# Encoder layer on one core: the first tile's queries projected alone, the other three tiles' queries behind its attention

## The chip, the cores and the metric

The kernel runs on one core of a Trainium2 chip. The time is the device time of one execution in microseconds (us). The kernel before was run three times: 1670.38, 1673.27 and 1676.81 us, median 1673.27 us.

## What is computed

One layer of a bidirectional encoder on 512 tokens of width 1024, float32. The part that the change touches is the mixer:

```python
hn = rms_norm(h, g_mix)
c_q, c_kv, k_r, q_d, k_d, v_d = split(hn @ w_in)          # 384, 256, 32, 512, 512, 512 columns
q  = rms_norm(c_q, g_cq) @ w_uq                           # 8 heads x 96, the last 32 with rope
kv = rms_norm(c_kv, g_ckv) @ w_ukv                        # keys and values of 8 heads
o_mla = softmax(q k^T) v                                  # all 512 keys
o_dil = dilated_attention(rope(q_d), rope(k_d), v_d)      # here: a bias and one softmax over 512 keys
h = h + concat(rms_norm(o_mla), rms_norm(o_dil)) @ w_out
h = h + peer_ffn(rms_norm(h))                             # top 16 of 128 x 128 experts for each of 8 heads
h = h + sigmoid(rms_norm(h) @ w_gate) * (p @ w_proj)
out = rms_norm(h)
```

Keys and values need all four tiles of 128 tokens. The queries of a tile are used by that tile's attention alone.

## The kernel before, in words

The 512 tokens are four tiles of 128; `ORDER = [1, 2, 3, 0]` is the order in which they go through attention ("first tile" below is tile 1, "last tile" is tile 0). One TensorE (PE) does all matrix work; VectorE (DVE), ScalarE (ACT) and GpSimd (POOL) do the rest; SyncE (SP) issues the loads.

**Projections** (L284 to L357). Five groups of columns of `w_in` in the order kv, kd, cq, qd, vd. A group has 8 chunks of 128 rows; each chunk's weights are loaded (`load_piece`), split into a high part on ACT and a low part on DVE (`w_step`, L186 and L188), and used by three matmuls for each of the four tiles (`mm_step`, L194). After a group its sums are evicted (L345 to L349), and a generator (`post_latent`, `post_dil`) goes on with them step by step (`run_posts`) between the next group's chunks: norm, rope, transposes, and for cq the product with `w_uq` (L250) and the transposes into `qT` (L259).

**Attention** (`attention`, L488). For each tile 8 steps of two heads: four with `qT` (L422), four with `qd` (L425). A step is `scores` (two matmuls, DVE reduction, ACT exponential), `weigh` (L442, L444), `flip` (L451, 8 transposes) two steps later and `values_` (L466) three steps later. `finish` (L482) ends a tile and starts its `after` generator: 8 pieces of `w_out` (L523), norm, transposes (L545), 8 pieces of `w_pq` (L562), products with the keys (L574). The pieces come through a ring of `WQB = 4` buffers. Between the steps of attention the loop takes one step of the oldest `after` and calls `fill(us)`, which takes steps from a list of background work `bg`.

**Background work.** When `after` of a tile ends it appends `topk` (L606: MAX, FIND_INDEX and MATCH_REPLACE on DVE, then decoding and a softmax) and, for tiles 1, 2 and 3, four `gates` (L686: one-hot products B on DVE, L713; matmuls, L724; eviction, L727; a store into `gD`). `topk` of a tile ends with three transposes on PE (L669, L670). The gates of the third tile are barred (`PRE`) until the dense stage.

**Dense stage** (from L870). For 128 rows of experts, matmuls h (L870) and y (L896) on the gated tiles. It starts when `bg` holds nothing but what is barred.

The built program's order on each engine is not the order of the code: a scheduler moves instructions of an engine past one another. So the order is shown below as it is built.

Of the kernel before, what the change touches and what calls it, by code (L numbers as in the profile page):

```python
# [52 lines left out]
WQB = 4  # L53
# [17 lines left out]
def encoder_kernel(ctx, tc, x, xT, pT, w_in, w_uq, w_ukv, w_out, w_pq, keysT, u, v, uT, vB, w_gate, w_proj,  # L71
# [7 lines left out]
    wk_s = ExitStack()  # L79
    wk = wk_s.enter_context(tc.tile_pool(name="wk", bufs=2))  # L80
# [4 lines left out]

    def t4(shape, name):
        return wk.tile(shape, F32, tag="t4", name=name, bufs=3)

    def t2(shape, name):
        return wk.tile(shape, F32, tag="t2", name=name, bufs=6)  # L90
# [3 lines left out]
    nTh = pj.tile([P, NC, T], FR, name="nTh", bufs=1)  # L94
    nTl = pj.tile([P, NC, T], FR, name="nTl", bufs=1)
# [3 lines left out]
    def load_piece(name, c):  # L99
        c0, c1 = WCOLS[name]  # L100
        w = pj.tile([P, 512], F32, tag="w", name="w", bufs=3)[:, :c1 - c0]
        nc.sync.dma_start(w, w_in[c * P:(c + 1) * P, c0:c1])
        raw[name, c] = w

    def norm_chunk(c):
        xc = t2([P, T], "xc")
        nc.sync.dma_start(xc, xT[c * P:(c + 1) * P, :])
        g = gc[:, G_MIX + c:G_MIX + c + 1]
        nc.scalar.activation(nTh[:, c, :], xc, AF.Copy, scale=g)
        nc.vector.scalar_tensor_tensor(nTl[:, c, :], xc, g, nTh[:, c, :].bitcast(F32), op0=OP.mult, op1=OP.subtract)  # L110
# [5 lines left out]
    io = wk.tile([P, NK], F32, name="io")  # L116
# [19 lines left out]

    def rstd_of(sq, small, src, width, pre=None):
        ss = small.tile([P, 3], F32, tag="ss", name="ss", bufs=8)
        nc.scalar.activation(sq, src, AF.Square, accum_out=ss[:, 0:1], scale=1.0 if pre is None else pre)
        nc.vector.tensor_scalar(ss[:, 1:2], ss[:, 0:1], 1.0 / width, EPS, op0=OP.mult, op1=OP.add)  # L140
        nc.gpsimd.tensor_tensor(ss[:, 2:3], ss[:, 1:2], nhalf, op=OP.pow)
        return ss[:, 2:3]

    def junk(width):
        return t2([P, 512], "sq").bitcast(BF)[:, :width]
# [36 lines left out]
    def w_step(name, c):  # L182
        w = raw.pop((name, c))
        n = w.shape[1]
        wh = pj.tile([P, 512], FR, tag="wh", name="wh", bufs=2)[:, :n]
        nc.scalar.activation(wh, w, AF.Copy)  # L186
        wl = pj.tile([P, 512], FR, tag="wl", name="wl", bufs=2)[:, :n]
# [3 lines left out]
    def mm_step(c, acc, wh, wl):  # L191
        for t in range(NT):
            for k, (l, r) in enumerate(((nTl, wh), (nTh, wl), (nTh, wh))):
                nc.tensor.matmul(acc[t], l[:, c, tok[t]], r, start=(c == 0 and k == 0),  # L194
                                 stop=(c == NC - 1 and k == 2))
# [3 lines left out]
    cqT = pj.tile([P, 3, T], F32, name="cqT", bufs=1)  # L199
    W = {}  # L200

    def post_latent(src, n, g0, dst, kr):
        lat = []
        for t in range(NT):
            c = src[t]
            r = rstd_of(junk(n * P), wk, c[:, :n * P], n * P)
            nc.vector.tensor_scalar(c[:, :n * P], c[:, :n * P], r, None, op0=OP.mult)
            if kr:
                rope(c[:, n * P:][:, None, :], rm[:, t], 1, 16)
        yield  # L210
        for t in range(NT):
            ps = tp1()
            for k in range(n):
                nc.tensor.transpose(ps[:, k, :], src[t][:, k * P:(k + 1) * P], ident)
            if kr:
                nc.tensor.transpose(ps[:KR, n, :], src[t][:, n * P:n * P + KR], ident)
            mul_g(dst[:, :, tok[t]], ps[:, :n, :], g0, n)
            if kr:
                nc.scalar.activation(krT[:, tok[t]], ps[:KR, n, :], AF.Copy)
            if t % 2:  # L220
                yield
        if kr:
            for h in range(NH):
                if h % 2:
                    nc.scalar.activation(kkT[HD:QK, h, :], krT, AF.Copy)
                else:
                    nc.vector.tensor_copy(kkT[HD:QK, h, :], krT)
            yield
            for hp in range(NH // 2):
                ps = tp1().rearrange("p a b -> p (a b)")  # L230
                for c in range(2):
                    nc.tensor.matmul(ps, W["ukv"][:, c, hp * P:(hp + 1) * P], ckT[:, c, :], start=(c == 0), stop=(c == 1))
                for a in range(2):
                    nc.scalar.activation(kkT[:HD, 2 * hp + a, :], ps[a * HD:(a + 1) * HD, :], AF.Copy)
                if hp % 2:
                    yield
            for t in range(NT):
                ps = tp1().rearrange("p a b -> p (a b)")
                for c in range(2):
                    nc.tensor.matmul(ps, ckT[:, c, tok[t]], W["ukv"][:, c, 512:], start=(c == 0), stop=(c == 1))  # L240
                nc.scalar.activation(vv[:, 0, t, :], ps, AF.Copy)
                if t % 2:
                    yield
        else:
            for t in range(NT):
                qt = t4([P, NH, QK], "qt")
                for s in range(2):
                    ps = tp1().rearrange("p a b -> p (a b)")
                    for c in range(3):
                        nc.tensor.matmul(ps[:, :384], cqT[:, c, tok[t]], W["uq"][:, c, s * 384:(s + 1) * 384],  # L250
                                         start=(c == 0), stop=(c == 2))
                    nc.scalar.activation(qt[:, 4 * s:4 * s + 4, :].rearrange("p h d -> p (h d)"), ps[:, :4 * QK],
                                         AF.Copy, scale=MLA_SCALE)
                rope(qt[:, :, HD:], rm[:, t], NH, 16)
                yield
                for s in range(2):
                    ps = tp1()
                    for h in range(4):
                        nc.tensor.transpose(ps[:QK, h, :], qt[:, 4 * s + h, :], ident)  # L259
                    nc.scalar.activation(qT[:QK, 4 * s:4 * s + 4, tok[t]], ps[:QK], AF.Copy)  # L260

    def post_dil(src, dst):
        for t in range(NT):
            rope(src[t].rearrange("p (h d) -> p h d", h=NH)[:, :, :16], rd[:, t], NH, 8)
            if t % 2:
                yield
        for t in range(NT):
            ps = tp1()
            for c in range(4):
                nc.tensor.transpose(ps[:, c, :], src[t][:, c * P:(c + 1) * P], ident)  # L270
            nc.scalar.activation(dst[:, :, tok[t]], ps, AF.Copy)
# [3 lines left out]
    seq = [(n, c) for n in ("kv", "kd", "cq", "qd", "vd") for c in range(NC)]  # L275
    pos_ = [0]

    def prefetch(k):
        for _ in range(k):
            if pos_[0] < len(seq):  # L280
# [7 lines left out]
    rm = pj.tile([P, NT, 2, 32], F32, name="rm", bufs=1)  # L288
    rd = pj.tile([P, NT, 2, 16], F32, name="rd", bufs=1)
# [7 lines left out]
    def r1_of(t):  # L297
        xt = t4([P, D], "xt")
        nc.sync.dma_start(xt, x[tok[t], :])
        r = rstd_of(junk(D), wk, xt, D)  # L300
# [12 lines left out]
    nxt = None  # L313
    for gi, name in enumerate(("kv", "kd", "cq", "qd", "vd")):
        n = WCOLS[name][1] - WCOLS[name][0]
        acc = [mm1()[:, :n] for _ in range(NT)]
        for c in range(NC):
            if nxt is None:
                nxt = w_step(name, c)
            cur = nxt  # L320
            prefetch(1)
            if gi == 0:
# [4 lines left out]
                if c == 4:  # L327
                    misc_loads()
            k = gi * NC + c + 1
            nxt = w_step(*seq[k]) if k < len(seq) else None  # L330
            mm_step(c, acc, *cur)
            run_posts()
        if gi == 0:
# [3 lines left out]
        if name == "vd":  # L337
            for t in range(NT):
                nc.scalar.activation(vv[:, 1, t, :], acc[t], AF.Copy, scale=r1[:, t:t + 1])
        else:  # L340
            ev = []
            for t in range(NT):
                e = pj.tile([P, 512], F32, tag="ev", name="ev", bufs=4)[:, :n]
                if name == "qd":
                    nc.vector.tensor_scalar(e, acc[t], r1[:, t:t + 1], -DIL_SCALE, op0=OP.mult, op1=OP.mult)  # L345
                elif t % 2:
                    nc.vector.tensor_scalar(e, acc[t], r1[:, t:t + 1], None, op0=OP.mult)
                else:
                    nc.scalar.activation(e, acc[t], AF.Copy, scale=r1[:, t:t + 1])  # L349
                ev.append(e)  # L350
            posts.append({"kv": lambda: post_latent(ev, 2, G_CKV, ckT, True),
                          "kd": lambda: post_dil(ev, kd),
                          "cq": lambda: post_latent(ev, 3, G_CQ, cqT, False),
                          "qd": lambda: post_dil(ev, qd)}[name]())
            run_posts()
    while posts:
        run_posts()  # L357
    pj_s.close()
    ps1_s.close()

    wk_s.close()

    tk_s = ExitStack()
# [7 lines left out]
    wa_s = ExitStack()  # L371
    wa = wa_s.enter_context(tc.tile_pool(name="wa", bufs=2))
    ps2_s = ExitStack()
    psum = ps2_s.enter_context(tc.tile_pool(name="psA", bufs=4, space=bass.MemoryType.PSUM))
# [835 lines left out]
```

## Time and profile before

| | us |
|---|---|
| median of 3 runs | 1673.27 |
| the profiled execution | 1674.36 |
| its span, on which all times of the trace lie | 1672.3 |
| PE busy in the span | 1604.1 (96%) |
| DVE busy | 1223.8 (73%) |
| ACT busy | 737.5 (44%) |
| POOL busy | 372.6 (22%) |

A busy share is an average over stages with different limits. So the stages are read apart: the trace has the projections from 0 to 149.7 us, attention with the `after` work and the background from there to the last `finish` at 415.4 us, a tail of `after`, `gates` and `topk` until the first dense matmul at 501.7 us, and the dense stage behind that. In the trace's rows "PEclk" is the clock granted to PE, as a share of 2.4 GHz; "PEld" is its weight loads, which run beside its matmuls.

### The profile page before, as it was taken

The numbers are of one execution on the slowest core, as the hardware profiler recorded it, in microseconds if no ns is written. First come the engines' busy times: TensorE is split into PE (matmuls) and PEld (weight loads), VectorE is DVE, ScalarE is ACT, GpSimd is POOL, SyncE is SP. The second block draws the span as 40 slices with busy tenths as digits, with TensorE's granted clock in tenths as the row PEclk, the third lists the DMA queues.
The fourth block names the chain that finished last, engine by engine and source line by source line (L and its number), as shares of the span: only waits on it lengthen the run. The fifth ranks groups of instructions, "written<-read, shape, count | busy, mean of one in ns | idle before, by whom it ended". The sixth has DMA issues, their size and how long they took to land.

```text
span 1672.3 us, 24854 instructions
## 1 busy us (share of the span) xinstructions
PE 1604.1 (96%) x9369; PEld 1405.3 (84%) x9369; DVE 1223.8 (73%) x2495; ACT 737.5 (44%) x1220; POOL 372.6 (22%) x302
## 2 busy tenths in 40 slices
PE   7999999999679989999999999999999999999998
PEld 6776777778669889999999999999999999999877
DVE  5235468796999867787887887788888888864566
ACT  5435655645446544433333333333333333333455
POOL 1000000000000001044444444444444444300000
PEclk9999999999889999999999999999999999999999
DMA  7212254375867667599999999999999999975511
GB/s 240 62 52 95 82 172 133 114 239 206 298 248 243 233 216 265 185 309 327 324 321 323 309 334 321 324 316 339 320 312 313 334 322 323 319 269 200 182 58 51
DMA packets 154088, 402.73 MB, mean 241 GB/s; under 512 B 13168, under 2 KB 64496, under 8 KB 152432
## 3 DMA queue, kind: packets, MB, share of 16 engines
q1 hardware_dynamic: 115232, 241.48, 43.4%
q0 software_dynamic: 36864, 134.23, 23.3%
q10 hardware_dynamic: 1872, 25.43, 3.9%
q8 instruction: 73, 1.20, 0.3%
q14 instruction: 47, 0.39, 0.1%
HBM read 369.64 MB, written 31.46 MB: 240 GB/s over the span
## 4 chain that ended last, share of the span: by engine, by line
PE 82%; DVE 11%; ACT 2%; DMA 2%; issue 1%; POOL 1%; SPq 0%; POOLq 0%; DVEq 0%; ACTq 0%
PE y L896 31%; PE h L870 31%; PE mm L194 4%; PE mm L523 2%; PE mm L562 2%; PE pg L965 2%; PE po L466 2%; PE gq L724 2%; DVE B L713 1%; PE tp L451 1%; PE mm L425 1%; PE mm L422 1%; PE tp L250 1%; DVE rep L595 1%; DVE hot L709 1%
## 5 line engine op out<-in xcount | busy, mean ns | idle before, releaser
L870 PE MATMUL h<-xTh,lo 128*128 128x384 f32 (+1 forms) x1024 | 340.3, 332 | 0.8 <-ACT gt L673 0.8
L870 PE MATMUL h<-xTh,hi 128*128 128x384 f32 (+1 forms) x1024 | 340.1, 332 | 0.0
L870 PE MATMUL h<-xTl,hi 128*128 128x384 f32 (+1 forms) x1024 | 339.0, 331 | 0.0
L774 POOL DMA_INDIRECT row<-in_u_dram,ei x128 | 165.9, 1296 | 449.2 <-DVE row L762 241.4
L896 PE MATMUL y<-hi,wl 128*128 128x512 f32 x768 | 241.4, 395 | 8.5 <-DVE wl L885 8.5
L896 PE MATMUL y<-lo,wh 128*128 128x512 f32 x768 | 238.9, 392 | 0.0
L896 PE MATMUL y<-hi,wh 128*128 128x512 f32 x768 | 238.4, 392 | 0.0
L774 POOL DMA_INDIRECT row<-in_v_dram,ei x128 | 182.5, 1426 | 208.5 <-DVE h L768 170.1
L819 DVE TENSOR_TENSOR lo<-v,hi 128x1024 fp32r<-128x1024 f32 x140 | 171.5, 1225 | 73.4 <-ACT hi L817 72.8
L879 ACT ACTIVATE w<-h 128x384 f32<-128x384 f32 (+2 forms) x140 | 65.0, 464 | 361.6 <-PE h L870 346.6
L870 PEld LDWEIGHTS h<-xTh,lo 128*128 128x128 f32 x1024 | 193.8, 189 | 5.8 <-ACT gt L673 1.1
L870 PEld LDWEIGHTS h<-xTl,hi 128*128 128x128 f32 x1024 | 193.8, 189 | 4.7
L870 PEld LDWEIGHTS h<-xTh,hi 128*128 128x128 f32 x1024 | 193.5, 189 | 0.0
L819 DVE TENSOR_TENSOR lo<-u,hi 128x1024 fp32r<-128x1024 f32 x128 | 156.8, 1225 | 46.0 <-ACT hi L817 44.5
L817 ACT ACTIVATE hi<-v 128x1024 fp32r<-128x1024 f32 x140 | 148.2, 1058 | 94.2 <-PE y L896 94.0
L896 PEld LDWEIGHTS y<-lo,wh 128*128 128x128 f32 x768 | 144.7, 188 | 32.3
L896 PEld LDWEIGHTS y<-hi,wh 128*128 128x128 f32 x768 | 144.6, 188 | 31.7
L896 PEld LDWEIGHTS y<-hi,wl 128*128 128x128 f32 x768 | 141.3, 189 | 30.4 <-DVE wl L885 9.8
L768 DVE SCALAR_TENSOR_TENSOR h<-row,hh,h 128x1024 f32<-128x1024 f32 x128 | 164.2, 1283 | 2.9
L762 DVE SCALAR_TENSOR_TENSOR row<-row,xg 128x1024 f32<-128x1024 f32 x128 | 150.2, 1221 | 0.0
L883 ACT ACTIVATE wh<-w 128x384 fp32r<-128x384 f32 (+2 forms) x140 | 69.6, 497 | 180.4 <-DVE w L881 179.0
L817 ACT ACTIVATE hi<-u 128x1024 fp32r<-128x1024 f32 x128 | 133.9, 1046 | 1.6 <-PE h L870 1.6
(255 smaller groups left out, 2249.5 us busy)
## 6 DMA issues: line engine op xcount, KB each, us to landing
u<-in_uT_dram SPq DMA_DIRECT2D x140, 512.0 KB
v<-in_vB_dram SPq DMA_DIRECT2D x140, 512.0 KB
gD<-stage ACTq DMA_DIRECT2D x12, 2048.0 KB
g<-gD SPq DMA_DIRECT2D x29, 768.0 KB
wq<-in_w_out_dram SPq DMA_DIRECT2D x32, 512.0 KB
wq<-in_w_pq_dram SPq DMA_DIRECT2D x32, 512.0 KB
w<-in_w_in_dram SPq DMA_DIRECT2D x24, 256.0 KB
wg<-in_w_gate_dram SPq DMA_DIRECT2D x8, 512.0 KB
```

The costliest lines, as they stand in the source:

```text
L194: nc.tensor.matmul(acc[t], l[:, c, tok[t]], r, start=(c == 0 and k == 0), stop=(c == NC - 1 and k == 2))
L466: nc.tensor.matmul(cx[t]["po"][a * HD:(a + 1) * HD, hp, :], vv[:, grp, c, h * HD:(h + 1) * HD], st[g][a][:, c, :], start=(c == 0), stop=(c ...
L523: nc.tensor.matmul(pss[grp][:, q * P:(q + 1) * P], mT[grp][:, c, :], w[:, grp * 4 + c, :], start=(c == 0), stop=(c == 3))
L762: nc.vector.scalar_tensor_tensor(row, row, 1.0, xg, op0=OP.mult, op1=OP.mult, accum_out=hh[:, k:k + 1])
L768: nc.vector.scalar_tensor_tensor(h0, row, hh[:, k:k + 1], h0, op0=OP.mult, op1=OP.add)
L774: nc.gpsimd.indirect_dma_start(out=row, out_offset=None, in_=v if w else u, in_offset=bass.IndirectOffsetOnAxis(ap=eis[s][:, kk:kk + 1], a ...
L817: nc.scalar.activation(hi, w, AF.Copy)
L819: nc.vector.tensor_sub(lo, w, hi.bitcast(F32))
L870: nc.tensor.matmul(ps, l[:, cs], r[:, c, ts], start=(c == 0 and k == 0), stop=(c == NC - 1 and k == 2))
L879: nc.scalar.activation(w, ps, AF.Gelu)
L883: nc.scalar.activation(wh, w, AF.Copy)
L896: nc.tensor.matmul(y[n][s], l[:, ts], r[:, s * 512:(s + 1) * 512], start=(first and k == 0), stop=(last and k == 2))
```

## The change

- The groups are now kv, kd (all four tiles), cq and qd for the first tile alone, vd (all tiles), and then cq and qd for the other three tiles. The last two (`rest_q`) run behind: one chunk to each step of the first tile's attention, then between the steps of the first tile's `after`. Their 16 chunks of weights are loaded and split again, `w_uq` is loaded again.
- The attention of the second tile starts when the rest is done (`open_rest`). Until then no gates are taken from `bg`.
- Buffers: in the rest `w`, `wh` have 2 and `wl`, `ab`, `qt`, `cqT` have 1; the `w_out`/`w_pq` ring has 3 in place of 4. PSUM in the first tile's attention and `after`: `mm` 2 banks, `tp` 2, `po` 1, `acc` 3; behind that a third `mm` bank (`mx`) and two for the gates. The normalized input is kept in two parts (`nT0` for the first tile, `nTr` for the others), so each chunk of it takes two ACT and two DVE instructions. `gates`' tiles move into a pool that opens with `open_rest`.

```diff
-WQB = 4
+WQB = 3
+    def now(many, few):
+        return (late[0], few) if late else (pj, many)
...
-    def mm_step(c, acc, wh, wl):
-        for t in range(NT):
-            for k, (l, r) in enumerate(((nTl, wh), (nTh, wl), (nTh, wh))):
+    def w_step(gi, c):
+        w = raw.pop((gi, c))
+        n = w.shape[1]
+        pool, k = now(2, 1)
+        wh = pool.tile([P, 512], FR, tag="wh", name="wh", bufs=2)[:, :n]
+        nc.scalar.activation(wh, w, AF.Copy)
+        wl = pool.tile([P, 512], FR, tag="wl", name="wl", bufs=k)[:, :n]
+        nc.vector.tensor_sub(wl, w, wh.bitcast(F32))
+        return wh, wl
+    def mm_step(c, acc, wh, wl, ts):
+        for ps, t in zip(acc, ts):
+            nh, nl = (of(t, a, b)[:, c, :] for a, b in zip(nT0, nTr))
+            for k, (l, r) in enumerate(((nl, wh), (nh, wl), (nh, wh))):
...
+    FIRST, REST = ORDER[:1], ORDER[1:]
+    GROUPS = ("kv", ALL), ("kd", ALL), ("cq", FIRST), ("qd", FIRST), ("vd", ALL), ("cq", REST), ("qd", REST)
...
+    for gi in range(5):
+        for _ in project(gi, mm1):
+            pass
     while posts:
         run_posts()
     pj_s.close()
+    late.append(qp_s.enter_context(tc.tile_pool(name="pq", bufs=2, side="right")))
+    W["uq"] = load_w(late[0], w_uq, 0, NH * QK, nc.sync, "uq", 1)
+    prefetch(2)
...
+    psum = psum_s.enter_context(tc.tile_pool(name="psA", bufs=2, space=bass.MemoryType.PSUM))
+    psq = psq_s.enter_context(tc.tile_pool(name="psq", bufs=3, space=bass.MemoryType.PSUM))
+    def mm_ps():
+        turn[0] += 1
+        if psx and turn[0] % 3 == 0:
+            return psx[0].tile([P, 512], F32, tag="mx", name="mm", bufs=1)
+        return psum.tile([P, 512], F32, tag="mm", name="mm")
+
+    def rest_q():
+        for gi in (5, 6):
+            yield from project(gi, lambda: psq.tile([P, 512], F32, tag="acc", name="acc"))
+            while posts:
+                run_posts()
+                yield True
...
-    for us in attention():
+    rest = rest_q()
+    barred.append(("gates", ORDER[0], 0))
+    for k, us in enumerate(attention(0, 8)):
+        if k % 4 == 3:
+            next(rest)
+        if k == 20:
+            fetch_w(WQB)
+    more = True
+    while more or afters:
+        for _ in range(2):
+            if afters:
+                step_after()
+                fill(FILL_A)
+        more = next(rest, None) is not None if more else False
+    open_rest()
+    barred.pop()
+    for us in attention(8, 8 * NT):
         if afters:
             step_after()
         fill(us)
```

How the built order moves, at the three places that the prediction speaks of.

DVE, in the middle of the first `topk`. Before, decoding (`eq`, L632, L635) stands among score reductions (L431) of a later tile:

```order
L632 TENSOR_TENSOR eq<-ab,iok 128x2048
L442 RECIPROCAL sm<-sm 128x2
L657 RECIPROCAL gs<-gs 128x4
L635 TENSOR_TENSOR eq<-eq,idb 128x2048
L431 TENSOR_REDUCE sm<-mm 128x1 x2
L483 TENSOR_SCALAR rg<-tp 128x1
```

Now, at the same place (`eq` is L683, L686, L690):

```order
L683 TENSOR_TENSOR eq<-ab,iok 128x2048
L204 TENSOR_TENSOR wl<-w,wh 128x512
L686 TENSOR_TENSOR eq<-eq,idb 128x2048
L483 TENSOR_REDUCE sm<-mm 128x1
L690 TENSOR_TENSOR eq<-eq 128x8x128
L204 TENSOR_TENSOR wl<-w,wh 128x512
L690 TENSOR_TENSOR eq<-eq 128x8x64
L709 TENSOR_TENSOR gd<-gd,gs 128x64
L690 TENSOR_TENSOR eq<-eq 128x8x32
L640 MAX vals<-sc 128x8
```

The last five of the rest's eight low-part splits for qd (L204) now stand behind the first half of the first `topk` and between its second half's instructions; in the kernel before, no split stands behind a `topk`.

DVE, at the last tile's second `finish` (`rg`). Before, behind it:

```order
L483 TENSOR_SCALAR rg<-tp 128x1
L658 TENSOR_TENSOR gd<-gd,gs 128x64
L639 TENSOR_TENSOR eq<-eq 128x8x32
L592 MAX_INDEX idx<-vals,sc 128x8
L641 TENSOR_TENSOR sel<-eq 128x128
L592 MAX_INDEX idx<-vals,sc 128x8 x2
L601 MAX_INDEX idx<-vals,rep 128x8 x4
L592 MAX_INDEX idx<-vals,sc 128x8 x4
```

Now, at it:

```order
L649 MAX top<-rep 128x8 x4
L652 MAX_INDEX pos<-top,rep 128x8 x4
L787 CAST dec<-pos 128x64
L535 TENSOR_SCALAR rg<-tp 128x1
L788 TENSOR_SCALAR p_4994<-pos 128x64
L791 TENSOR_SCALAR dec<-dec 128x64
L789 CAST dec<-p_4994 128x64
L704 TENSOR_TENSOR gd<-top 128x64
```

The searches of the third tile's first half (MAX, FIND_INDEX, MATCH_REPLACE), which stood partly behind the last `finish`, now stand ahead of it.

PE, just ahead of the dense stage. Before:

```order
L724 MATMUL gq<-hot,B 128x128
L574 MATMUL mm<-kbd,qp 128x256 x3
L669 MATMUL gq<-ident,i1t 128x128 x2
L670 MATMUL gq<-ident,gd 128x128
L870 MATMUL h<-xTh,lo 128x256
```

Now:

```order
L775 MATMUL gq<-hot,B 128x128
L613 MATMUL mm<-xTt,wq 128x128 x29
L625 MATMUL mm<-kbd,qp 128x256 x4
L613 MATMUL mm<-xTt,wq 128x128 x15
L720 MATMUL tp<-ident,i1t 128x128 x2
L721 MATMUL tp<-ident,gd 128x128
L613 MATMUL mm<-xTt,wq 128x128 x17
L625 MATMUL mm<-kbd,qp 128x256 x4
L937 MATMUL h<-xTh,lo 128x256
```

The third tile's transposes (L720, L721) stood last before the dense matmuls; now 17 matmuls with `w_pq` and 4 with the keys stand between.

## Rows read from the trace of the kernel before

**Rows 1.** Busy time by stage (the "windows" view), PE and DVE above all.

```profile
core 0: us, PE busy (x) PEld busy (x) DVE busy (x) ACT busy (x) POOL busy (x), PEclk, DMA share, GB/s
0.00:149.70 149.70, 138.56 (x648) 108.62 (x648) 56.86 (x158) 65.25 (x127) 8.63 (x26) 1.00 0.35 106
149.70:187.00 37.30, 36.94 (x256) 22.48 (x257) 27.11 (x60) 31.14 (x75) 0.69 (x3) 1.00 0.24 85
187.00:234.00 47.00, 46.54 (x369) 37.66 (x369) 17.17 (x41) 23.93 (x53) 1.65 (x3) 1.00 0.57 174
234.00:325.00 91.00, 86.51 (x669) 69.55 (x666) 73.55 (x394) 51.44 (x107) 2.02 (x3) 0.98 0.43 137
325.00:415.40 90.40, 83.72 (x756) 69.85 (x754) 72.51 (x241) 51.59 (x111) 5.24 (x3) 0.92 0.58 200
415.40:501.70 86.30, 60.61 (x559) 56.12 (x559) 83.97 (x331) 38.03 (x72) 1.64 (x2) 0.85 0.74 271
```

**Rows 2.** Chain that ended last, PE in cq and qd: start, us, what, records.

```profile
71.92 8.36 PE mm L194 x48
...
115.05 3.87 PE tp L250 x12
118.92 2.75 PE mm L194 x12
```

**Rows 3.** PE's instructions in order of time, first tile's attention.

```profile
149.71 5.56 PE L422 MATMUL mm<-kkT,qT 96*128 96x512 f32 x12 [0.78 <-ACT vv L339]
155.11 1.04 PE L451 MATMUL tp<-ident,pr 128*128 128x128 f32 x8
...
161.53 1.09 PE L466 MATMUL po<-prT,vv 128*64 128x128 f32 x16
162.56 1.09 PE L451 MATMUL tp<-ident,pr 128*128 128x128 f32 x8
163.58 1.13 PE L425 MATMUL mm<-kd,qd 64*128 64x512 f32 x4
```

**Rows 4.** Groups by line and shape, 0 to 200 us: busy us, mean ns, idle before.

```profile
L188 DVE TENSOR_TENSOR wl<-w,wh 128x512 fp32r<-128x512 f32 x24 | 16.6, 690 | 35.2 <-ACT wh L186 35.2
L186 ACT ACTIVATE wh<-w 128x512 fp32r<-128x512 f32 x24 | 15.1, 630 | 37.9 <-PE mm L194 35.8 <-DVE ev L180 2.1
L188 DVE TENSOR_TENSOR wl<-w,wh 128x384 fp32r<-128x384 f32 x8 | 4.5, 557 | 14.2 <-ACT wh L186 14.2
L186 ACT ACTIVATE wh<-w 128x384 fp32r<-128x384 f32 x8 | 4.2, 526 | 11.3 <-PE mm L194 11.3
L259 PE MATMUL tp<-ident,qt 128*96 128x128 f32 x32 | 4.1, 272 | 0.0
L175 DVE TENSOR_TENSOR ab<-ev,rd 128x128 f32<-128x128 f32 x8 | 2.3, 285 | 3.7 <-ACT ev L349 3.7
```

**Rows 5.** DVE's instructions in order of time, first half of the first topk.

```profile
234.05 0.87 DVE L589 MAX8 vals<-sc 128x8 f32<-128x128 f32 x4 [0.32 <-ACT sc L575]
...
252.89 1.21 DVE L632 TENSOR_TENSOR eq<-ab,iok 128x2048 bf16<-128x2048 bf16 x1
```

**Rows 6.** Waits of PE, 285 to 415.4 us: total us, times, longest.

```profile
PE tp L545 <- DVE hn L538: 1.9, 1, 1.9
PE tp L545 <- DVE xTt L158: 2.4, 1, 2.4
PE gq L724 <- DVE B L713: 2.0, 1, 2.0
```

**Rows 7.** Three windows around one of these waits, columns as in the first group.

```profile
365.00:370.00 5.00, 2.76 (x22) 1.39 (x18) 4.57 (x10) 3.29 (x7) 0.40 (x1) 1.00 0.91 369
370.00:375.00 5.00, 4.86 (x17) 3.04 (x17) 5.00 (x32) 0.00 (x0) 0.00 (x0) 0.57 0.75 262
375.00:380.00 5.00, 5.00 (x53) 4.14 (x52) 2.20 (x4) 2.63 (x7) 0.00 (x0) 0.75 0.02 3
```

**Rows 8.** Groups by line and shape, 200 to 502 us, PE.

```profile
L562 PE MATMUL mm<-xTt,wq 128*128 128x128 f32 x512 | 65.7, 283 | 0.0
L574 PE MATMUL mm<-kbd,qp 128*128 128x256 f32 x64 | 16.5, 392 | 1.1 <-ACT qp L566 1.1
```

More of the change, by code (lines that the diff above doesn't have):

```diff
@@ L135, in encoder_kernel, with of @@
     qd = att.tile([P, 4, T], F32, name="qd")
+    def of(t, first, rest):
+        k = ORDER.index(t)
+        return rest[:, :, (k - 1) * P:k * P] if k else first
     def rstd_of(sq, small, src, width, pre=None):
@@ L144, in junk @@
     def junk(width):
-        return t2([P, 512], "sq").bitcast(BF)[:, :width]
+        pool, n = now(2, 1)
+        return pool.tile([P, now(0, 384)[1] or D], BF, tag="jk", name="sq", bufs=n)[:, :width]
     def tp1():
@@ L197, in encoder_kernel @@
     ckT = pj.tile([P, 2, T], F32, name="ckT", bufs=1)
     krT = pj.tile([KR, T], F32, name="krT", bufs=1)
-    cqT = pj.tile([P, 3, T], F32, name="cqT", bufs=1)
+    rm = pn.tile([P, NT, 2, 32], F32, name="rm", bufs=1)
+    rd = pn.tile([P, NT, 2, 16], F32, name="rd", bufs=1)
     W = {}
[L202 to L209, printed above, removed]
+    ALL = list(range(NT))
@@ L262, in post_dil @@
-    def post_dil(src, dst):
+        for h in range(NH):
+            if h % 2:
+                nc.scalar.activation(kkT[HD:QK, h, :], krT, AF.Copy)
+            else:
+                nc.vector.tensor_copy(kkT[HD:QK, h, :], krT)
+        yield
+        for hp in range(NH // 2):
+            ps = tp1().rearrange("p a b -> p (a b)")
+            for c in range(2):
+                nc.tensor.matmul(ps, W["ukv"][:, c, hp * P:(hp + 1) * P], ckT[:, c, :], start=(c == 0), stop=(c == 1))
+            for a in range(2):
+                nc.scalar.activation(kkT[:HD, 2 * hp + a, :], ps[a * HD:(a + 1) * HD, :], AF.Copy)
+            if hp % 2:
+                yield
@@ L275, in encoder_kernel, with post_cq @@
-    seq = [(n, c) for n in ("kv", "kd", "cq", "qd", "vd") for c in range(NC)]
+    def post_cq(src, ts):
+        for t, c in zip(ts, src):
+            scale_latent(c, 3)
+            yield
+            cqT = now(0, 0)[0].tile([P, 3, P], F32, tag="cqT", name="cqT", bufs=1)
+            ps = tp1()
+            for k in range(3):
+                nc.tensor.transpose(ps[:, k, :], c[:, k * P:(k + 1) * P], ident)
+            mul_g(cqT, ps[:, :3, :], G_CQ, 3)
+            yield
+            qt = t4([P, NH, QK], "qt")
+            for s in range(2):
+                ps = tp1().rearrange("p a b -> p (a b)")
+                for k in range(3):
+                    nc.tensor.matmul(ps[:, :384], cqT[:, k, :], W["uq"][:, k, s * 384:(s + 1) * 384],
+                                     start=(k == 0), stop=(k == 2))
+                nc.scalar.activation(qt[:, 4 * s:4 * s + 4, :].rearrange("p h d -> p (h d)"), ps[:, :4 * QK],
+                                     AF.Copy, scale=MLA_SCALE)
+            rope(qt[:, :, HD:], rm[:, t], NH, 16)
+            yield
+            for s in range(2):
+                ps = tp1()
+                for h in range(4):
+                    nc.tensor.transpose(ps[:QK, h, :], qt[:, 4 * s + h, :], ident)
+                nc.scalar.activation(qT[:QK, 4 * s:4 * s + 4, tok[t]], ps[:QK], AF.Copy)
+            yield
@@ L276, in encoder_kernel @@
+    seq = [(gi, c) for gi in range(len(GROUPS)) for c in range(NC)]
     pos_ = [0]
@@ L311, in run_posts, with project @@
                 posts.pop(0)
-    nxt = None
-    for gi, name in enumerate(("kv", "kd", "cq", "qd", "vd")):
+    ahead = []
+    def project(gi, ps_of):
+        name, ts = GROUPS[gi]
         n = WCOLS[name][1] - WCOLS[name][0]
-        acc = [mm1()[:, :n] for _ in range(NT)]
+        acc = [ps_of()[:, :n] for _ in ts]
         for c in range(NC):
-            if nxt is None:
-                nxt = w_step(name, c)
-            cur = nxt
+            if not ahead:
+                ahead.append(w_step(gi, c))
+            cur = ahead.pop()
             prefetch(1)
@@ L486, in finish, with attention @@
             afters.append(after(t, cx[t]["mT"], rr))
-    def attention():
+    def attention(G0, NG):
         def at(g):
             return g, ORDER[g // 8], g % 8 // 4, g % 4
-        NG = 8 * NT
-        for g in range(NG + 4):
+        for g in range(G0, NG + 4):
             if g < NG:
```

228 lines of the change are left out of this document (103 added, 125 removed).

## The prediction

> **What bounds the kernel now.** I read the busy time by stage first. [rows 1] The reader should see PE busy for 138.56 of 149.7 us in the projections, 36.94 of 37.3 in the first tile's attention and 46.54 of 47.0 in the stretch behind it: up to 234 us PE is the bound and has almost nothing to give. From 234 to 415.4 us it loses a little, partly as idle time (4.5 and 6.7 us), partly through a lower clock (0.98 and 0.92). From 415.4 to 501.7 us the bound is another: DVE is busy 83.97 of 86.3 us and PE only 60.61. The chain of waits says the same of the projections: it runs through PE's matmuls. [rows 2] Then I read PE's instructions one by one. [rows 3] In the middle of the first attention each begins where the last ends (161.53, 162.56, 163.58): no gap. The dense stage behind 501.7 us keeps its order, so its length is taken as unchanged; the time moves by as much as the first dense matmul does.
>
> **What is moved.** Three of four tiles of cq and qd leave the front. For cq that is 8 chunks x 3 tiles x 3 matmuls = 72 of 8.36 / 48 = 0.174 us, 12.5 us; for qd 72 of 2.75 / 12 = 0.229 us, 16.5 us; the product with w_uq three times 3.87 us, 11.6 us [rows 2]; and 45 transposes of 4.1 / 32 = 0.128 us, 5.8 us [rows 4]. Together 46.4 us of PE. Attention starts earlier by that, at about 103 us plus stalls. The work itself isn't removed. PE had 0.4 + 0.5 us free up to 234 us, so the rest's matmuls lengthen the first attention and its `after` by about what the front gave up: 0 net.
>
> The first topk doesn't need the rest. Its searches began at 234.05 us [rows 5] and now come some 38 us earlier: the 46 less what part of the rest's matmuls already stands ahead of them.
>
> **What it costs**, term by term.
>
> (a) Feeding the first tile's cq and qd. PE has 3 matmuls to a chunk instead of 12: 8 x 3 x (0.174 + 0.229) = 9.7 us. DVE needs 8 x (0.557 + 0.690) = 10.0 us for the same 16 splits [rows 4] beside the posts. If the posts of kd fill PE's gaps, this costs nothing; if the split on ACT and that on DVE followed one another for each chunk, 8 x (1.083 + 1.320) = 19.2 us, 9.5 more than PE has. I take +4 (0 to 9): two buffers let ACT and DVE overlap, but DVE has the ropes too.
>
> (b) The second split: 16 ACT instructions, 8 x (0.526 + 0.630) = 9.2 us, and 10.0 us of DVE [rows 4], in stretches where ACT was busy 31.14 of 37.3 and 23.93 of 47 us, DVE 27.11 and 17.17 [rows 1]. The reload is 3.7 MB of `w_in` and 1.2 MB of `w_uq`, some 37 GB/s over 130 us, where the DMA share was 0.24 to 0.57 [rows 1]. SP only issues loads; they queue ahead of the ring's pieces. With three ring buffers two pieces of 16 x 65.7 / 512 = 2.05 us each [rows 8] still cover a load, and before PE's longest waits were for DVE, not for a piece. 0 (0 to 3). The norm's chunks in two instructions: 0, beside the load of kv's weights (0 to 2).
>
> (c) The start of attention. Before, six score matmuls (5.56 us) covered the reduction, exponential and weighing ahead of the first flip at 155.11 us [rows 3]. With two `mm` banks four stand there, 3.7 us: +2 (0 to 5, a whole chain uncovered).
>
> (d) Five low-part splits of qd behind the first topk on DVE, with one `wl` buffer. The first waits for the half topk: 18.8 us from the first MAX to `eq` [rows 5], while PE comes to that chunk some 1 to 3 us sooner. After it DVE spends about 2.5 to 3.2 us between two splits (an `eq` of 1.21 us [rows 5], a reduction and the split's 0.690 [rows 4]) where PE has only 9 x 0.229 = 2.06 us to do: up to 1.1 x 4. Then eviction, rope and transposes of three tiles with little of the rest left to cover them. Behind the waiting matmuls stands all of PE's queue: the pieces of `after`, whose end opens the second tile's attention. Below 2 it can't be, since the order puts the split behind the topk's half; 16 is every one of these uncovered, ropes included (0.285 each [rows 4]). I take +9.
>
> (e) The second tile's attention starts with an empty pipeline, its reductions in DVE's queue among the topk: +2 (0 to 5), as (c).
>
> (f) Between 187 and 415.4 us PE lost, by busy time times clock, 228.4 - (46.54 + 86.51 x 0.98 + 83.72 x 0.92) = 20.1 us [rows 1]. What the order covers of it: the two waits of 1.9 and 2.4 us in `after`'s norm [rows 6], beside which gate matmuls or rest matmuls now stand, and one clock drop, 0.57 and 0.75 of full speed over two windows of 5 us, which cost 2.1 + 1.2 = 3.3 us [rows 7]. -7 (-12 to +5, if others come for them).
>
> Here a rule and the row differ in extent. The row shows PE idle for 2.24 of 5 us and then at 0.57 of its clock, so partly at the 1.2 GHz level; yet over all of 234 to 325 us, with a wait of 1.9 us inside, the clock was 0.98 [rows 1, 6]. The Trainium skill ("TensorE: Matmul & The Clock Gate", "HAM oscillation — how this bites in real kernels") says that a loop whose matmuls are shorter than its wait starts cold again at every turn. By that rule each of the waits of (d) would bring its clock drop too; this trace agrees for one wait and not for the other.
>
> (g) The tail. Ahead of the last `finish` stand about 12 us more of DVE's searches than before, so DVE's 84 us behind it become 72. But the last order excerpt puts 17 matmuls with `w_pq` and 4 with the keys behind the third tile's transposes, 17 x 0.128 + 2.06 = 4.3 us [rows 8], and with what feeds them some 6.5 us. -5 (-12, nothing of it uncovered, to +3).
>
> Sum: 4 + 0 + 2 + 9 + 2 - 7 - 5 = +5. The profiled execution took 1674.36 us, so 1679.4 us; that execution lies 1.1 us above the median of 1673.27. Own range of this case 1668 to 1692: the terms' ends won't all come together. About 0.5% is what a measurement can tell from no change, here 1664.9 to 1681.6 us.
>
> **Rivals.**
>
> *R1: the background fills the stages (faster).* The earlier topk gives PE gate matmuls in every later wait, all of the 20.1 us of (f) go and the whole 12 us of DVE in (g). For it: DVE was busy only 17.17 of 47 us just before 234 us [rows 1], so there the searches cost nothing. Against: gates are held back until the rest is done, and PE's total is the same. With the costs of (a), (c), (d), (e) as taken, 17 - 20 - 12 = -15: 1659 us; with their low ends 1644.
>
> *R2: the rest's feed becomes the bound (slower).* `wl` has one buffer and its writer stands in a queue with topk. If PE's waits there last over about 2 us they bring the clock down, 3.3 us each as at 370 us [rows 7]; five splits so, 16.5 us on top: 1696 us. It decides from the point where DVE needs over 4 us between two splits, not 3. For it: DVE's queue in order, `eq` instructions of 1.21 us and searches in front of each split. Against: PE's queue has `after` pieces between the chunks.
>
> *R3: the first attention has room.* If PE isn't full there, the 12.5 us of cq fit in for nothing: 1667 us. Against it the starts without a gap [rows 3]; for it, weight loads are busy only 22.48 of 37.3 us, 60% [rows 1]. The Trainium skill ("Perfetto Trace Analysis", "Identifying the Most-Contended Engine") calls the matmuls' busy share a bad measure of headroom, and that of weight loads a good one; by it 40% would be free here. The rows bear it out only as far as those loads go: the 4 score records take 1.13 us however full the loads are.
>
> That the change doesn't do what it says can be left out: the order shows cq and qd of three tiles behind the attention's start.
>
> **How the numbers follow.** Chances: the forecast 0.50, R1 0.28, R2 0.13, R3 0.09. Faster by over 0.5%: R1 0.24, R3 0.04, the forecast's low end 0.03, together 0.31. Slower: R2 0.13 and the part of the forecast over 1681.6 us, 0.19, together 0.32. Same: 0.37. The range 1652 to 1696 us leaves out R1's lower third (0.10) and 0.08 above.
>
> **What would show it.** Right: attention begins at 105 to 112 us and the first MAX near 196 us; PE waits for `wl` some 5 times, 1 to 4 us each; the second tile's attention starts near 235 us; the last `finish` falls at 415 to 428 us, DVE is busy 72 to 75 us behind it, and the first dense matmul comes at 500 to 512 us. Wrong towards R1: hardly a wait for `wl`, PE's clock near 1.00 until the last `finish`, and that `finish` before 405 us. Wrong towards R2: the clock under 0.9 in the rest's second half and the second tile's attention after 250 us. Wrong towards R3: PE's steps in the first attention no longer than 3.1 us with the rest's matmuls in them. And everything here is wrong if the dense stage, whose weights now lie elsewhere in memory, is longer or shorter by more than 2 us.

## The result, and the profile after

The changed kernel took 1689.36 us (median of 4 runs, 1688.61 to 1690.19), the kernel before beside it 1674.36. Its ratio to the kernel before is 1.0102, 95% interval [1.0081, 1.0123]: 1% slower. The forecast was 1679.4 us, +0.3% of the profiled execution, with 1652 to 1696 as its range. Range and sign of the sum hold; the size doesn't (15 us and not 5), and the place where most of the time went is one that the sum had at nothing.

First the stages of the changed kernel ("windows" view, columns as in [rows 1], and cut at the same events: start of attention, first `finish`, first MAX, last `finish`, first dense matmul).

```profile
0.00:111.60 111.60, 98.01 (x423) 71.75 (x424) 46.74 (x129) 56.98 (x112) 7.03 (x23) 1.00 0.46 144
111.60:157.80 46.20, 45.45 (x314) 32.45 (x315) 28.18 (x61) 30.03 (x69) 1.23 (x3) 1.00 0.38 125
157.80:200.40 42.60, 41.08 (x282) 34.82 (x280) 11.83 (x27) 10.09 (x22) 2.16 (x4) 1.00 0.62 195
200.40:428.10 227.70, 214.84 (x1677) 165.18 (x1676) 179.65 (x761) 138.42 (x294) 4.57 (x7) 0.99 0.41 140
428.10:517.20 89.10, 65.22 (x559) 60.04 (x558) 80.50 (x276) 38.45 (x72) 1.09 (x2) 0.85 0.81 297
```

Attention begins at 111.6 us where it began at 149.7, the first MAX comes at 200.4 us instead of 234.05 [rows 5]: attention is moved as forecast, the MAX by 33.7 us where some 38 were. The dense matmuls begin at 517.2 us instead of 501.7, 15.5 us later; behind them the kernel is 1 us shorter (1169.6 against 1170.6). So the whole loss lies ahead of the dense stage. The last row is the surprise: DVE has less to do there than before (80.5 of 89.1 us; 83.97 of 86.3 [rows 1]) and the stretch is longer all the same.

What PE waited for says why. PE's waits up to 520 us (the "waits" view: total us, times, longest), the lines that matter:

```profile
PE gq L775 <- DVE B L764: 11.3, 7, 3.8
PE mm L613 <- DMA wq<-in_w_pq_dram: 7.5, 2, 4.5
PE mm L211 <- ACT ev L377: 2.0, 1, 2.0
PE mm L574 <- DMA wq<-in_w_out_dram: 1.6, 3, 0.8
PE acc L211 <- DVE wl L204: 1.5, 2, 1.1
```

The second and the fourth line are waits for pieces of `w_out` and `w_pq`, 9.1 us in five waits, from the ring that shrank from 4 buffers to 3. The kernel before has one wait for a piece, of 5.0 us in its tail, which its view puts down to ACT. Two rows of SP's order of time, and the row of PE:

```profile
426.27 0.33 SPq L802 DMA_DIRECT2D u<-in_uT_dram  x1
426.70 2.02 SPq L389 DMA_DIRECT2D wq<-in_w_out_dram  x4
...
431.40 9.36 PE L523 MATMUL mm<-wq,mT 128*128 128x128 f32 x64 [5.01 <-ACT d L677]
```

The first of these four loads lands at 431.26 us by its semaphore in the trace, just ahead of the matmul, and the matmul doesn't read the `d` that the view names. This wait isn't the ring's depth: the first piece's buffer was free at about 420.6 us (PE's 64 matmuls began at 418.75 us, 1.83 us for each piece), but the load stood on SP behind a load for the dense stage (`u`), which waited for DVE until 426.3 us. In the changed kernel the loads with the long waits are issued as soon as their buffer comes free. One of them, in PE's order of time:

```profile
322.98 1.95 PE L613 MATMUL mm<-xTt,wq 128*128 128x128 f32 x16
325.91 3.84 PE L613 MATMUL mm<-xTt,wq 128*128 128x128 f32 x32
332.80 3.31 PE L613 MATMUL mm<-xTt,wq 128*128 128x128 f32 x14 [3.05 <-DMA wq<-in_w_pq_dram]
```

Three pieces run (16 matmuls each), and the fourth isn't there. The windows around it, columns as in [rows 1]:

```profile
322.00:327.00 5.00, 5.00 (x40) 4.12 (x38) 5.00 (x10) 3.51 (x10) 0.00 (x0) 1.00 1.01 399
327.00:332.00 5.00, 2.75 (x25) 2.56 (x23) 0.83 (x4) 0.00 (x0) 0.00 (x0) 1.00 0.98 398
332.00:338.00 6.00, 5.20 (x40) 5.09 (x40) 0.96 (x2) 1.41 (x3) 0.00 (x0) 0.72 0.36 144
```

The DMA share is full (1.01 and 0.98) while the load is under way, and after the wait PE's clock is down to 0.72. The second long wait lies in the tail. The chain that ended last there (start, us, what, records):

```profile
485.70 1.55 PE gq L775 x16
487.26 2.26 PE mm L613 x10
489.53 8.03 DMA wq<-in_w_pq_dram
497.60 3.79 PE mm L613 x16
...
502.07 3.78 PE mm L625 x8
505.85 3.76 PE mm L613 x30
```

```profile
497.60:502.00 4.40, 3.78 (x16) 3.48 (x16) 1.08 (x1) 0.58 (x2) 0.00 (x0) 0.50 0.49 198
```

A buffer comes free at 489.5 us, its load lands 8.0 us later, and the 16 matmuls behind it run at 0.50 of full speed, the 1.2 GHz level: 3.79 us where a piece takes 2.05 [rows 8]. Before, the tail ended with DVE. Now it ends with the last tile's pieces, on PE.

### The profile page after: what moved, and what is told of

It is laid out like the page before. It is cut to its first block, busy times and chain, and to the rows that moved or that the text cites. A ratio compares the mean times of both kernels' runs of the same rounds, so it can differ in the third digit from the quotient of the medians.

```text
span 1686.8 us, 24980 instructions
## 1 busy us (share of the span) xinstructions
PE 1614.4 (96%) x9369; PEld 1404.0 (83%) x9369; DVE 1236.2 (73%) x2519; ACT 747.3 (44%) x1244; POOL 368.4 (22%) x302
## 4 chain that ended last, share of the span: by engine, by line
PE 80%; DVE 10%; DMA 4%; ACT 3%; issue 1%; POOL 0%; SPq 0%; POOLq 0%; DVEq 0%; ACTq 0%
PE y L963 31%; PE h L937 30%; PE mm L211 3%; PE mm L574 2%; PE mm L613 2%; PE pg L1032 2%; PE po L518 2%; PE gq L775 1%; PE mm L474 1%; PE tp L503 1%; PE acc L211 1%; DVE B L764 1%; DMA wq<-in_w_pq_dram 1%; DMA wq<-in_w_out_dram 1%; PE h L940 1%
## 5 line engine op out<-in xcount | busy, mean ns | idle before, releaser
L885 DVE TENSOR_TENSOR lo<-u,hi 128x1024 fp32r<-128x1024 f32 x128 | 156.8, 1225 | 46.4 <-ACT hi L883 46.4
```

Source lines behind the costliest of these rows:

```text
L885: nc.vector.tensor_sub(lo, w, hi.bitcast(F32))
```

## The experiments

Theory S: the loss is the sum of many stalls (the front's feed, starts with an empty pipeline, the order of the tail). Theory R: it is the ring. The kernel before was run again beside each group of runs (medians 1672.3, 1672.9 and 1674.7 us), so ratios to it are given.

**The ring alone, in the kernel before.**

```diff
-WQB = 4
+WQB = 3
```

> The kernel before with the ring of w_out and w_pq pieces cut from 4 buffers to 3, nothing else. Theory S (stalls and order): the ring costs little by itself, because the pieces in the tail run between gate matmuls; 1673 to 1677 us, and no wait of PE for a piece over 1 us. Theory R (the ring): most of the +15 us comes from the ring; 1681 us or more, with waits of PE for pieces of 3 to 8 us in the tail.

1682.08 us, ratio 1.0048 [1.0031, 1.0064]: R's side (1681 us or more). By the ratio it is 8 us for one buffer. PE's waits in it:

```profile
PE mm L562 <- DMA wq<-in_w_pq_dram: 7.3, 2, 3.9
PE mm L523 <- DMA wq<-in_w_out_dram: 6.9, 2, 6.6
```

Three of the four lie in the last 80 us ahead of the dense stage (at 433, 477 and 495 us). The one at 433 us, 6.6 us long, has its counterpart in the 5.0 us of the kernel before; the two for `w_pq` have none. S expected none over 1 us: S is wrong on this point.

**A fourth buffer in the changed kernel.** There is no room for it beside the rest's buffers, so it is opened with `open_rest`, and `hn` is written over `ht` to make room.

```diff
+            nw[0] += 1
+            if wx and nw[0] % 4 == 0:
+                w = wx[0].tile([P, NC, P], F32, tag="wx", name="wq", bufs=1)
+            else:
+                w = wa.tile([P, NC, P], F32, tag="wq", name="wq", bufs=WQB)
...
         gate_sb[0] = wa_s.enter_context(tc.tile_pool(name="wg", bufs=2))
+        wx.append(wa_s.enter_context(tc.tile_pool(name="wx", bufs=1)))
+        fetch_w()
...
-        hn = ht if t == ORDER[0] else gate_sb[0].tile([P, D], F32, tag="hn", name="hn", bufs=1)
+        hn = ht
```

> The changed kernel with a fourth buffer of the ring from the second tile's attention on (the room for it comes from writing hn in place). Theory R expects the wait of 4.5 us for a piece and the low clock behind it (24 matmuls at half speed, some 4 us) to go: 1681 us (1679 to 1684). Theory S expects a part of it, since the last tile's chain is late for the order of its pieces: 1684 to 1689 us.

1675.67 us, ratio 1.0013 [0.9997, 1.0028]: under R's range of 1679 to 1684, and far under S's. The waits for `w_pq` are gone; of the kind this is left, 4.3 us of it at 450 us in the tail:

```profile
PE mm L581 <- DMA wq<-in_w_out_dram: 5.1, 3, 4.3
```

The second tile ends at the same time in both profiles (its second `finish` at 287.1 and 287.0 us), the third tile's first at 333.5 against 338.8 us, the last at 425.0 against 430.5, and the dense matmuls begin at 507.5 against 517.2. So the ring took 5.3 us at the wait shown at 332 us and 4.3 us in the tail. The two profiled executions are 11.5 us apart; most of the rest, 1.7 us, lies in the dense stage.

**Its control: hn over ht, three buffers.**

```diff
-        hn = ht if t == ORDER[0] else gate_sb[0].tile([P, D], F32, tag="hn", name="hn", bufs=1)
+        hn = ht
```

> The changed kernel with hn written in place, and the ring left at 3: the part of the run with four buffers that is not the ring. Theory R (the ring of 3 is the largest cost of the change, some 14 us) expects what the changed kernel took, 1687 to 1691 us. The rival, that the place of hn made the difference, expects 1680 us or less.

1686.24 us, ratio 1.0080 [1.0058, 1.0101]. The median lies just under the 1687 expected, its interval overlaps with that of the changed kernel. What is left between this run and the one with four buffers is the ring alone: 0.0067 of 1673, 11 us, give or take 4 by the intervals. Against the changed kernel itself it is 0.0089, 15 us, with the place of `hn` in it. So the ring is 11 to 15 of the 15 to 17 us lost. The change shrinks other buffers too (`mT` from 3 to 2, `sq` and `qp` from 2 to 1); no run tests them, and with the ring of four 0.1% is left to explain.

**Two buffers, in the kernel before (one run).**

```diff
-WQB = 4
+WQB = 2
```

> The kernel before with a ring of two, one look. A load lands in about 4.3 us and a piece's 16 matmuls take 2.05 us, so with two buffers one piece covers half a load: up to 2.2 us for each piece that runs without work between. If the ring is a wait of that kind its price rises fast from 4 to 3 to 2 buffers: 20 us or more over the kernel before, with waits of PE for pieces of 30 us or more in sum. If the 8 us of the ring of three came from another order of instructions, about 8 us again.

1686.81 us, 12 us over the kernel before. The price is 8 and then about 12 us; by a single run the rise isn't clear of the noise. The 20 us expected were too many: probably the attention steps and gate matmuls between the pieces cover much of what a second buffer less costs, which no run shows. The waits by name come to 23.8 us, where 30 or more were expected:

```profile
PE mm L562 <- DMA wq<-in_w_pq_dram: 18.0, 6, 7.1
PE mm L523 <- DMA wq<-in_w_out_dram: 5.8, 5, 2.9
```

**The rest ahead of attention.**

```diff
-    for k, us in enumerate(attention(0, 8)):
-        if k % 4 == 3:
-            next(rest)
+    for _ in rest:
+        pass
+    for k, us in enumerate(attention(0, 8)):
...
-    more = True
+    more = False
```

> The changed kernel, with all of the rest (cq and qd of the other three tiles, split a second time) run ahead of the first attention instead of between its steps; the order of the tail is the same. Theory S says that the front's feed costs 6 to 8 us and interleaving another 7 (switches between kinds of matmuls, empty pipelines at two starts of attention): this run keeps the first and loses the second, about 1682 us (1679 to 1685). The rival, that interleaving earns what it costs through the earlier topk, expects 1689 us or more here.

1712.08 us, ratio 1.0226 [1.0195, 1.0256]: 21 us slower than the changed kernel, on the rival's side (1689 or more) and far past it. The stretch from the first tile's last `finish` to its first MAX shows most of the reason:

```profile
203.20:240.00 36.80, 26.20 (x185) 24.28 (x185) 6.12 (x10) 2.08 (x4) 1.09 (x2) 0.86 0.62 205
```

In the changed program the first tile's `after` runs out before the second attention opens, and without the rest's matmuls beside it PE is busy 26.2 of 36.8 us at a clock of 0.86. So the run doesn't price interleaving against the kernel before, where the second attention fills that stretch; it shows that in this program the rest is the filling, and that S's 7 us for interleaving was a wrong account.

**Less gate work between the last tile's pieces.**

```diff
-FILL_A, FILL_B, FILL_D = 0.8, 3, 2
+FILL_A, FILL_B, FILL_D = 0.8, 1, 2
```

This one edit was made in three kernels. In the changed kernel:

> The changed kernel with FILL_B 1 in place of 3: in the tail the last tile's w_out and w_pq pieces run with less gate work between them, and the third tile's transposes stand last again, as before. Theory S says that the tail ended with the last tile's chain (norm at 473 us, w_pq at 481 to 514) and that DVE's 78.6 us of work would end earlier: dense starts 8 us sooner, 1681 us (1678 to 1685), and PE's wait of 4.5 us for a w_pq piece is gone. The rival, that DVE's work bounds the tail whatever the order, expects 1687 to 1691 us.

1688.46 us, ratio 1.0091 [1.0064, 1.0117]: nothing. PE's wait for `w_pq` grew from 7.5 us in two waits to 9.8 in three (3.2 us at 330 us as before, 4.1 and 2.5 in the tail), so the pieces that now stood together met the ring. With the fourth buffer:

> Ring of four and FILL_B 1 together. With three buffers FILL_B 1 gave nothing, and PE waited 9.8 us for pieces there. If that was the ring's doing, the two together let the tail end with DVE's work: 4 us under the ring of four alone, 1672 us (1669 to 1674). The rival, that the order of the tail is worth nothing, expects 1674 to 1677 us.

1670.82 us, ratio 0.9988 [0.9976, 1.0000], against 1.0013 with the fourth buffer alone. The order of the tail is worth 4 us once the ring lets it. The first dense matmul then waits for the third tile's decoding again, as in the kernel before:

```profile
499.49 0.58 PE L944 MATMUL h<-xTh,lo 128*128 128x256 f32 x1 [4.12 <-ACT gt L731]
```

And in the kernel before, as a control:

> The kernel before with FILL_B 1 alone: what that number is worth without the change. If its 4 us belong to the changed order of the tail, nothing here: 1671 to 1675 us. If any kernel of this kind gains by it, 1669 us or less.

1683.35 us, ratio 1.0062 [1.0042, 1.0082]: slower, which neither side expected. Its dense matmuls begin where they began before (501.3 and 501.7 us); PE then is busy 187.4 us of the next 199, where it was 193.8 before. The trace has the loss in the first 19 us of them, where PE is busy 12.1 of 18.8 us (18.3 of 18.3 before): it waits 3.6 us for a product B of the gates and 3.1 us for a split of the dense stage, both from DVE. Why DVE is late with them was not followed.

**Splits of the front two chunks ahead**, with the fourth buffer.

```diff
-        pool, k = now(2, 1)
-        wh = pool.tile([P, 512], FR, tag="wh", name="wh", bufs=2)[:, :n]
+        pool, k = now(3, 1)
+        wh = pool.tile([P, 512], FR, tag="wh", name="wh", bufs=max(2, k))[:, :n]
...
-            if k < len(seq) and (seq[k][0] < 5) == (gi < 5):
-                ahead.append(w_step(*seq[k]))
+            while len(ahead) < (2 if gi < 5 else 1) and k + len(ahead) < len(seq) and seq[k + len(ahead)] in raw:
+                if (seq[k + len(ahead)][0] < 5) != (gi < 5):
+                    break
+                ahead.append(w_step(*seq[k + len(ahead)]))
```

> Ring of four, and in the front three buffers for the high and low parts of the weights with the splits two chunks ahead. Theory: the first tile's cq and qd lose 4 us because their splits come one chunk ahead; with two ahead, 2 us of it go, attention begins at 108.5 us and the whole takes 1673 to 1674 us. The rival, that DVE's work in that stretch (splits and ropes) is the limit, expects no change against the ring of four, 1675.5 us, with attention at 110.8 us.

1671.56 us, ratio 0.9995 [0.9983, 1.0007], 3 us under the fourth buffer alone, and attention at 106.0 us instead of 110.8. In the stretch of the first tile's cq and qd 1.8 us of the 4.8 are gained (19.6 us instead of 21.5), about the 2 expected; the other 2.9 lie ahead of it, in kv and kd (cq's first matmul comes at 62.60 us instead of 65.54). So splits made too late were a part of the price of the short groups. Whether DVE's amount of work is the rest was not shown.

**The tile of x first**, with the fourth buffer.

```diff
-                if c > 5:
+                if c > 6:
                     prefetch(1)
```

> Ring of four, and one chunk of weights fewer loaded ahead of the last tile of x in the projections of kv. Theory: kd's first matmuls wait 2.8 us at 24 to 32 us because kv's evictions stand on ACT behind a square that waits for its tile of x; with x earlier, 2 us of it go: attention at 109 us, 1674 us. The rival, that the tile of x comes no sooner or that vd's end takes the gain back, expects 1675.5 us.

1675.36 us, ratio 1.0016 [1.0002, 1.0029]: no gain, and kd's first matmuls still wait 2.0 us for the eviction. The order of that one load isn't the cause; what is, stays open. (In the run with the deeper split these waits are 0.4 and 0.5 us.)

**All three together.** The fourth buffer, FILL_B 1 and the deeper split:

> Ring of four, FILL_B 1 and the deeper split of the front together. If the 4 us of each are gains at different places (the front and the tail) they add up: 1667 us (1665 to 1669), 0.3% under the kernel before. If both only shift the same wait, 1670 to 1672 us.

1666.50 us, ratio 0.9957 [0.9941, 0.9973]: the gains add up, and the kernel is 0.4% faster than the kernel before. Its tail (last `finish` to first dense matmul, columns as in [rows 1]):

```profile
421.00:496.73 75.73, 56.47 (x546) 52.98 (x544) 73.70 (x252) 33.16 (x61) 1.10 (x2) 0.89 0.76 288
```

75.7 us long and DVE busy for 73.7 of them: with the pieces on time DVE bounds the tail once more, and with ten microseconds less to do than in [rows 1].

**The rest sooner**, on top of that.

```diff
-    while more or afters:
-        for _ in range(2):
+    while more:
+        for _ in range(1):
```

> As the run with both, and between the steps of the first tile's attention's end and its `after` the rest takes one step to each step of `after` instead of one to two, and the second tile's attention opens when the rest is done, whatever is left of that `after`. Theory: PE loses 8 us between 216 and 246 us because the last posts of qd and the start of the second attention have nothing beside them; with w_pq and key matmuls left beside them 4 us of it go, 1663 us (1661 to 1666). The rival, that these waits are bound by DVE's queue among the topk, expects 1667 us.

1667.16 us, ratio 0.9958 [0.9943, 0.9973]: the same. The second tile is sooner (its first `finish` at 251.6 instead of 255.4 us, its second at 275.4 instead of 281.6), and the third tile's first comes at 330.2 instead of 327.8 us: all of it is given back there. The rival holds in its number; whether DVE's queue is the reason was not shown.

## Why the prediction was right and wrong

That the time lies in the range is luck: the ring was put at nothing and took 11 us or more, the front took 4 us more than its term, and other terms that were set too high made up for a part.

**Right: what moves.** Attention was to begin at 105 to 112 us and began at 111.6; the second tile's scores were due near 235 us and come at 234.3, apart from four matmuls that the scheduler put among the rest's (216.5 and 220.8 us). The first MAX was due near 196 us and came at 200.4, the last `finish` at 415 to 428 and came at 430.5: both miss. That PE's work is moved and not removed is seen in the first attention, where a step grew by what was put into it. The starts of its flips:

```profile
125.37 1.09 PE L503 MATMUL tp<-ident,pr 128*128 128x128 f32 x8
...
130.25 1.09 PE L503 MATMUL tp<-ident,pr 128*128 128x128 f32 x8
...
135.12 1.09 PE L503 MATMUL tp<-ident,pr 128*128 128x128 f32 x8
```

They are 4.88 and 4.87 us apart: 3.1 as before [rows 3], nine matmuls of 0.174 us, and 0.2 more. So R3 falls: there was no room. The Trainium skill's rule ("Perfetto Trace Analysis", "Identifying the Most-Contended Engine") that weight loads tell the headroom better would have had 40% free there, and this trace disagrees with it: loads were busy 32.45 of 46.2 us, and the step grew by the full price of the matmuls.

**(a), the front: sized too small.** +4 was taken and about 8 came: attention begins 8.3 us behind the 103.3 us that the 46.4 leave. Of these 2.5 lie ahead of cq, whose first matmul comes at 66.20 us and came at 63.74: the first matmul of all is 0.7 us later (6.60 against 5.93), and kd's first matmuls wait 2.8 us for evictions instead of 0.9. Behind it the way to attention shrank from 86.0 to 45.4 us, by 40.6 and not by 46.4. Of the missing 5.8 us 1.3 are the transposes: 45 were priced by their mean busy time, 0.128 us [rows 4], and follow each other every 0.1 us, so less was moved. Some 4.5 us are left for the feed itself, as priced.

**(b), the ring at nothing: the step that failed.** "Two pieces of 2.05 us each still cover a load": two pieces are 4.1 us, and the prediction set no landing time beside them. Its other ground, that PE's longest waits before were for DVE and not for a piece, was read up to 415.4 us [rows 6]; the 5.0 us at 431.4 us stand behind that. In the changed kernel a piece's load takes this long from issue to landing:

```profile
DMA to landing us min/median/max: 3.3/4.3/10.4
```

The median alone is over the cover, and for the two loads behind the long waits it is 7.8 and 8.0 us, with the DMA share near 1.0. With three buffers two long waits arise (3.05 and 4.46 us), each with a lower clock behind it, and the pieces of the last tile end later for it. By the runs that is 11 to 15 us, the largest single term of the change, where the prediction had 0 to 3.

**(c), the start of attention: sized too large.** +2 was taken; PE waited there once, 0.74 us for an exponential, at 114.3 us.

**(d), the splits behind the topk: sized too large.** +9 was taken. PE waited for `wl` twice, 1.5 us in all, and twice for the ropes of qd behind them, 2.0 us. The last chunks come 2.4 to 4.3 us apart instead of 2.06, but the scheduler had put the second tile's first scores into two of these gaps. This error hid a part of the other: with 11 to 15 us for the ring and 3.5 for (d) the sum would have been +10.5 to +14.5, 1685 to 1689 us.

**(e) and (f).** Counted as in the prediction, PE lost 42.6 + 227.7 - (41.08 + 214.84 x 0.99) = 16.5 us between the first `finish` and the last, 20.1 before. That is 3.6 us less, with (d), (e) and the ring's first wait (5.3 us by the fourth buffer's run) in it; +4 was forecast for (d), (e) and (f) together. So by this account PE's other gaps shrank by more than the 7 us taken. That the topk's earlier start is what fills them fits, but no run shows it. Where the rest ends and the second attention starts, PE waits for a rope, and then, as the pipeline of the second attention fills, for an exponential:

```profile
232.22 0.66 PE L293 MATMUL tp<-ident,ev 128*128 128x128 f32 x4 [1.50 <-DVE ev L195]
...
238.39 2.84 PE L474 MATMUL mm<-kkT,qT 96*128 96x512 f32 x6 [1.36 <-ACT pr L484]
```

The clock is down between the two, behind the waits for the ropes (from 234 to 236 us it was 0.50):

```profile
216.00:222.00 6.00, 4.90 (x18) 2.99 (x17) 6.00 (x15) 1.74 (x4) 0.00 (x0) 1.00 0.15 44
...
234.00:240.00 6.00, 4.64 (x13) 2.31 (x12) 4.93 (x25) 3.53 (x9) 0.00 (x0) 0.76 0.00 0
```

**The clock.** R2 priced a clock drop for each of five waits for `wl`. Behind the two that came (1.1 and 0.4 us) there was none: the first, at 218 us, left the clock at full speed (the first of the two rows above). Drops came behind the ropes and behind the ring's waits: 0.72 after 3.05 us idle and 0.50 after 4.46. The tail has others, behind waits of the gates' matmuls for DVE: after 4.43 us idle 16 of them take 1.87 us at 470.1 us, where 16 took 1.06 at 463.3. The kernel before has such drops too; its tail's clock is 0.85 [rows 1], as in the changed kernel. The Trainium skill ("TensorE: Matmul & The Clock Gate", "HAM oscillation — how this bites in real kernels") says that a loop whose matmuls take less time than its wait for the next load starts cold again at every turn. The trace agrees in kind for the ring's two waits, though they are single waits and no loop.

**(g), the tail.** -5 was taken, and the stretch from the last `finish` (`rg` on DVE, 430.5 us) to 517.2 took 86.7 us, 1.5 more than the 85.2 before. That searches moved ahead of the `finish` was right, but DVE is busy 78.1 us behind it and not 72 to 75. What stands behind the third tile's transposes took 6.8 us (509.8 to 516.6), close to the 6.5 priced, and that by luck: a matmul with `w_pq` in the built order is two records of the trace, so the 17 are 34 records and 4.1 us, not 2.2. The loss lies ahead of these transposes: the load of 8 us and half the clock behind it made the last tile's pieces the end of the stage. The wait reaches DVE too. ACT's eviction of the late piece's sums (`qp`) stands in its queue ahead of an exponential of the third tile (`gd`), and DVE waits for that:

```profile
501.42 0.60 ACT L617 ACTIVATE qp<-mm 128x512 f32<-128x512 f32 x1 [10.60 <-PE mm L613]
501.91 0.25 ACT L705 ACTIVATE gd<-gd 128x64 f32<-128x64 f32 x1
...
502.19 0.22 DVE L707 TENSOR_REDUCE gs<-gd 128x4 f32<-128x64 f32 x1 [3.51 <-ACT gd L705]
```

Freed of the ring and put in the old order the stretch takes 75.7 us.

**R1** is seen in part. The idle time it spoke of is there to be had: 1666.5 us is within reach of its 1659. But it isn't had by this change, which took the buffer that it needed; and the fourth buffer alone (ratio 1.0013) doesn't give it either, without the order of the tail and the deeper split.

## What to carry to other kernels

A ring's depth is priced by landing time against the work between two uses of a buffer, and both have to be read where they are worst: the median load of a quiet stretch says nothing about a stretch where stores and prefetches fill the DMA engines. That PE hardly waits for a load in the profile of before (once, for a load held up on SP) means that the ring is deep enough, not that it is one too deep. And a wait that a view puts down to another engine can still be a load's: what the instruction reads, and when the load was issued, tell. When memory is taken from one place to make another earlier, compare the two in the same units first: here one buffer of the ring (512 KB, 4 KB in each partition) was worth 11 us, and the reordering with this buffer and two further edits 7.

## What the runs showed of the hardware that was not expected

The same 512 KB load took 3.3 us at best and 10.4 us at worst within one execution, the worst from 290.1 us on, where the DMA share was 0.98 (290.0 to 300.5 us). And a wait of 4.5 us cost PE nearly twice its length: the piece behind it took 3.79 us instead of 2.05 [rows 8], and the keys' matmuls behind that 3.78 us, where the same eight took 1.99 us at 429.6 us, at full speed. That is 3.5 us on top of the wait.
